# One K panel instead of two in combined form in the up projection of a streaming encoder layer

## Chip, cores and metric

The kernel runs on one core of a Trainium2 chip. The metric is the device time of one execution in microseconds (us). Engines are named as in the profile: PE is TensorE (matmuls; PEld its weight loads), DVE is VectorE, ACT is ScalarE, POOL is GpSimd, SP is SyncE, which here only issues loads.

## What is computed

One layer of a hybrid encoder for 256 prompt frames of one stream and 16 frames each of 8 sample streams (384 rows in all, three tiles of 128): projections, a convolution branch and an attention branch, their gated sum through `w_out`, and then the part in which the change lies, a feed-forward block with a gated causal convolution:

```
h2 = rmsnorm(x, norm_ffn_g)
up = h2 @ w_up                      # 384 x 2048 times 2048 x 11264
g_half = up[..., :D_FF]             # D_FF = 5632
u_half = up[..., D_FF:]
ext_f = concatenate([ffn_buf, g_half], axis=1)
gc = causal_dwconv(ext_f, ffn_dw_w, ffn_dw_b)      # 3 taps
x = x + (silu(gc) * u_half) @ w_down
```

The last gate rows of each stream are outputs too (`prompt_ffn`, `sample_ffn`).

## The kernel before

**Precision and units.** A product of two float32 matrices is made of three matmuls: both operands are split into a high part and the rest (`hi`, `lo`), and hi·hi, hi·lo and lo·hi are added up in PSUM (L1154 to L1156, and L301 to L303 in `gemm`). A weight block of 256 rows by 512 columns (512 KB) is loaded by SP into a raw buffer (`fetch`, L127), and `split` (L146) makes its halves: `hi` on ACT (L155), then `lo` on DVE (L156), which frees the raw buffer. There are five raw buffers in the feed-forward block (three named `raw`, and S0 and S1 of an older pool) and three pairs of `hi` and `lo` (two and `third`). `ahead` (L255) keeps up to `depth` splits issued ahead of their matmuls. Every engine works through its own queue in order; a scheduler sets the order within a queue by priorities at build time.

**The up projection** runs in 11 column groups (`up_group`, L1165). Group g makes 512 gate columns and 512 up columns of all 384 rows. K = 2048 is cut into four panels q of 512, each of two halves of 256. The groups alternate with the down projection: up 0, 1, 2, down, up 3, 4, down, and so on, so that the profile has five up stages (of 3, 2, 2, 2 and 2 groups).

**Plain panels** take their four weight blocks as they are: `pu0`, `pu1` (up columns, K halves 0 and 1) and `pg0`, `pg1` (gate columns), each for three row tiles and two K tiles of 128. One such item is 18 matmuls, a panel 72.

**Panels in combined form** (`MIXED = (0, 1)`) use a scheme of Strassen's kind for the 256 prompt rows. With the four blocks B11, B21 (gate columns, K halves 0 and 1) and B12, B22 (up columns), seven products take the place of eight. The items, in the code's names:

| item | what is split | loads | products | matmuls |
|---|---|---|---|---|
| b22 | B22 | B22 | q3, sample up | 12 |
| t3 | sums = B22 + B12 (L197) | B12 | p7, sample up | 12 |
| t1 | B11 + B12, in place (L202) | B11 | p5 | 6 |
| b11 | B11 | B11, a second time | p1, sample gate | 12 |
| t2 | sums = sums + B11 (L206) | | q6 | 6 |
| b21 | B21 | B21 | sample gate, p2 | 12 |
| t4 | sums = sums + B21 (L206) | | q4 | 6 |

The 128 sample rows have four plain products in these items. A panel is 66 matmuls, five loads and seven splits. The activations' combinations (`xm`) are made once, after `w_out`. q3, p2 and q4, and the up rows' second accumulator q2, go on to collect the plain panels; p5, p7, p1 and q6 are combined with them when they leave PSUM, on ACT and DVE (L1190 to L1225). There are five PSUM banks for these (`acc`) and three more (`misc`).

**After a group,** the up rows and the gate rows are turned to columns (DVE transposes L315, POOL's DMAs L320 and L325 through DRAM), the gate rows get their taps (L1124, L1126), and `product` (L1132 to L1136) makes the halves for the down projection. These follow in `tick`s, one for every nine matmuls.

`steps` (L172) sets the order of a group's items. In groups 1 to 10 the items of the panels 0 and 1 are spread among the eight plain ones; group 0 takes the six up items of both panels first.

Of the kernel before, what the change touches and what calls it, by code (L numbers as in the profile page):

```python
# [33 lines left out]
SPLIT_AHEAD, EVAC_AHEAD, FFN_AHEAD = 150, 60, 250  # L34
MIXED = (0, 1)

# [5 lines left out]
def hybrid_step(  # L42
# [23 lines left out]
    gp, close_gp = pool("acts")  # L66
    acc, close_acc = pool("acc", bufs=5, space=PSUM)
# [56 lines left out]

    fetched, wide = [], [False]
# [18 lines left out]
    third = []  # L144

    def split(raw, o, by_row=False):  # L146
        if third and len(third) % 3 == 0:
            hi, lo = third[0]
# [3 lines left out]
        if third:  # L152
            third.append(0)
        for k in (slice(0, 1), slice(1, 2)) if by_row else (slice(0, 2),):
            nc.scalar.copy(hi[:, k, :o], raw[:, k, :o])  # L155
            tt(lo[:, k, :o], raw[:, k, :o], f(hi[:, k, :o]), op=ALU.subtract)  # L156
        return hi, lo
# [14 lines left out]
    def steps(first):  # L172
        def spread(heavy, plain):
            n, m = len(heavy), len(plain)
            return [x for i in range(n) for x in [heavy[i]] + plain[i * m // n:(i + 1) * m // n]]

        up = [(what, q) for q in MIXED for what in ("b22", "t3", "t1")]
        top = [(what, q) for q in MIXED for what in ("b11", "t2")]
        low = [(what, q) for q in MIXED for what in ("b21", "t4")]
        pu, pg = ([(f"p{side}{h}", q) for q in PLAIN for h in range(2)] for side in "ug")  # L180
        if first:
            return up + pu[:-2] + top[:-2] + pu[-2:] + top[-2:] + spread(low, pg)
        return spread(up, pu) + spread(top + low, pg)

    def planned_mixed(w, c1, c2, first):
        held = {}

        def add(fn):
            plan.append(lambda: split(fn(), 512))

        def single(name, k, c):
            held[name] = fetch([rows_of(w, k, c, 512)])[0]
            return held[name]

        def both(q):
            sums[q] = new_sum[0](q)
            tt(sums[q], held["b22"][:], single("b12", 4 * q, c2)[:], op=ALU.add)  # L197
            return sums[q]

        def top(q):  # L200
            b = single("b11", 4 * q, c1)
            tt(b[:], b[:], held["b12"][:], op=ALU.add)  # L202
            return b

        def grown(q, name):
            tt(sums[q], sums[q], held[name][:], op=ALU.add)  # L206
            return sums[q]

        make = {"b22": lambda q: single("b22", 4 * q + 2, c2), "t3": both, "t1": top,
                "b11": lambda q: single("b11", 4 * q, c1), "t2": lambda q: grown(q, "b11"),  # L210
                "b21": lambda q: single("b21", 4 * q + 2, c1), "t4": lambda q: grown(q, "b21")}
        for what, q in steps(first):
            if what[0] == "p":
                planned(w, 4 * q + 2 * int(what[2]), [({"u": c2, "g": c1}[what[1]], 512)], 2)
            else:
                add(lambda what=what, q=q: make[what](q))
# [61 lines left out]
    def gemm(jobs, sides=()):  # L278
        for js in jobs:
# [4 lines left out]
            for j, k in [(j, k + i) for k in range(0, js[0]["nk"], 2) for j in js for i in range(2)]:  # L284
# [19 lines left out]
                if sp:  # L304
                    with tc.high_priority(offset=FFN_AHEAD if wide[0] else EVAC_AHEAD):
                        for m in range(nb):
                            j["evac"](m, ps[m])
                    if "done" in j:
                        j["done"]()
# [661 lines left out]
    p_x2, close_x2 = pool("x2")  # L971
    third_parts = [p_x2.tile([P, 2, 512], F32R, name=n)[:] for n in ("hi3", "lo3")]
    xg = {q: p_x2.tile([P, 2, 4, NT], F32R, name=f"xg{q}") for q in range(4) if q not in MIXED}
# [15 lines left out]

    def block():  # L990
        return p_w.tile([P, NTT * 512], F32, tag="block", bufs=4, name="block")

# [89 lines left out]
    plain_sums = gp.tile([P, 3, 2, 512], F32, tag="G0", name="sums")  # L1082
    third.append(third_parts)
# [6 lines left out]
    def up_g_done(g, box):  # L1090
        def done():
            cs = slice(512 * g, 512 * (g + 1))
            rows = box[0].rows
# [3 lines left out]
            gd = box[0].moved().rearrange("p i t q c -> p (i t) q c")  # L1097

# [44 lines left out]

    def run(seq, forms, finish):
        last = {b: (i, n) for i, prods in enumerate(seq) for n, (b, _, _) in enumerate(prods)}
        for i, prods in enumerate(seq):
            ahead(depth[0])
            hi, lo = ready.pop(0)
            for n, (b, (ah, al), kk) in enumerate(prods):
# [6 lines left out]
                mm(o, al, hi[:, kk, :], start=False, stop=last[b] == (i, n))  # L1156
            for b in last:
                if last[b][0] == i:
                    finish[b](forms[b][:])
            spent[0] += len(prods)  # L1160
# [4 lines left out]
    def up_group(g):  # L1165
# [12 lines left out]
        def rows(name):  # L1178
            if name not in box:
                for n in ("u", "g"):  # L1180
                    box[n] = block()[:].rearrange("p (t n) -> p t n", t=NTT)
            return box[name]

        def out(fn):
# [4 lines left out]

        def p5(ps):  # L1190
            nc.scalar.activation(e0, ps, AF.Identity, scale=scale[0])
            nc.scalar.activation(e1, ps, AF.Identity, scale=scale[1])

        def p7(ps):
            nc.scalar.activation(rows("g")[:, 1], ps, AF.Identity, scale=scale[1])  # L1195

        def q3(ps):
            stt(rows("u")[:, 0], ps, scale[0], e0, op0=ALU.mult, op1=ALU.subtract)

        def q2(ps):  # L1200
            u = rows("u")[:, 1]
            with tc.high_priority(offset=FFN_AHEAD):
                stt(u, ps, scale[1], e1, op0=ALU.mult, op1=ALU.subtract)
            tt(u, u, rows("g")[:, 1], op=ALU.subtract)
# [4 lines left out]
        def p1(ps):  # L1209
            nc.scalar.copy(e1, ps)  # L1210
            nc.scalar.activation(rows("g")[:, 0], ps, AF.Identity, scale=scale[0])

        def q6(ps):
            with tc.high_priority(offset=FFN_AHEAD):
                tt(e0, ps, e1, op=ALU.subtract)
            for r, sc in ((rows("u")[:, 0], scale[0]), (rows("u")[:, 1], scale[1]),
                          (rows("g")[:, 1], nr2[:, 1:2])):
                stt(r, e0, sc, r, op0=ALU.mult, op1=ALU.add)
            ups[g] = Turned(block, rows("u")).moved().rearrange("p i t q c -> p (i t) q c")

# [3 lines left out]
        def q4(ps):  # L1224
            stt(rows("g")[:, 1], ps, scale[1], rows("g")[:, 1], op0=ALU.mult, op1=ALU.add)  # L1225

# [4 lines left out]
               if what[0] == "p" else pairs(q, *made[what]) for what, q in steps(g == 0)]  # L1231
        run(seq, forms, dict(p5=out(p5), p7=out(p7), q3=out(q3), q2=q2, tu=sample("u"),
                             p1=out(p1), q6=q6, p2=out(p2), q4=out(q4), tg=sample("g")))
        up_g_done(g, [Turned(block, rows("g"))])()

# [81 lines left out]
```

## Time and profile before

| what | us |
|---|---|
| median of 3 runs | 2016.13 (2009.7 to 2018.01) |
| the profiled execution | 2013.98 |
| its span, first to last instruction | 2012.3 |
| five up stages begin at | 912.4, 1185.5, 1384.3, 1581.0, 1778.8 |
| five down stages begin at | 1120.2, 1319.0, 1515.8, 1713.5, 1909.7 |

The mean clock granted to TensorE is 0.997 of full speed. In the profile, a group of instructions has its line, engine and operation, output and inputs by the program's names, count, busy time and mean, then the idle time of its engine just before, and what ended it. A row of the timeline has start, length, engine, line, and in brackets the wait ahead of it. A row of waits has the waiter, what it waited for, total, count, longest. A row of windows has the stretch, its length, and each engine's busy time with its count of instructions.

### The profile page before, as it was taken

Reading aid. Unit: us, or ns where it says so; the run is one execution under the profiler, and the core shown is the slowest. Engines: PE = TensorE matmul, PEld = TensorE weight load, DVE = VectorE, ACT = ScalarE, POOL = GpSimd, SP = SyncE. Lnnn points to the kernel's source line nnn. Section 1 sums busy time; section 2 is a strip of 40 time slices with the busy share of each in tenths; the row PEclk is TensorE's granted clock in tenths of the full one; section 3 lists DMA queues with packets and bytes.
Section 4 is the critical chain, followed back from the end, with each engine's and each line's share of the span. In section 5 each row is a group of like instructions: output and inputs, shape, how many; then the busy total and the mean of one; then the engine's idle time right before and its main releaser. Section 6 shows DMA issues by size and latency. Waiting matters only on the chain.

```text
span 2012.3 us, 24838 instructions
## 1 busy us (share of the span) xinstructions
PE 1972.1 (98%) x9254; PEld 1649.8 (82%) x9254; DVE 1267.4 (63%) x1692; ACT 893.4 (44%) x1308; POOL 261.0 (13%) x527
## 2 busy tenths in 40 slices
PE   9999999999999999999899999999999999999999
PEld 9999888888888888887777887788778877887787
DVE  4478889646556356557588647754775467556853
ACT  5433354554426223455355534543454445443541
POOL 1001121100000002101121200230112012201210
PEclk9999999999999999999999999999999999999999
DMA  6555776664444458667655775576557655776563
GB/s 182 159 170 158 234 226 216 203 178 133 129 126 126 128 179 269 207 215 217 202 154 184 209 201 158 167 218 198 164 175 221 188 182 163 219 209 192 171 204 115
DMA packets 200884, 369.74 MB, mean 184 GB/s; under 512 B 16738, under 2 KB 66909, under 8 KB 200755
## 3 DMA queue, kind: packets, MB, share of 16 engines
q1 hardware_dynamic: 178763, 284.32, 45.2%
q0 software_dynamic: 21680, 83.70, 14.8%
q8 instruction: 72, 1.18, 0.2%
q14 instruction: 49, 0.40, 0.1%
q10 hardware_dynamic: 320, 0.14, 0.0%
HBM read 313.32 MB, written 55.24 MB: 183 GB/s over the span
## 4 chain that ended last, share of the span: by engine, by line
PE 76%; DVE 10%; DMA 9%; issue 3%; ACT 1%; POOL 1%; DVEq 0%; SPq 0%; POOLq 0%
PE acc L301 17%; PE acc L302 17%; PE acc L303 17%; DMA raw<-in_w_up_dram 7%; DVE lo L156 5%; PE acc L1155 4%; PE acc L1156 4%; PE acc L1154 4%; PE misc L1156 2%; PE misc L1155 2%; PE misc L1154 2%; PE acc L298 2%; PE acc L296 1%; PE acc L297 1%; DVE ut L566 1%
## 5 line engine op out<-in xcount | busy, mean ns | idle before, releaser
L155 ACT CAST hi<-raw 128x1024 fp32r<-128x1024 f32 (+2 forms) x481 | 498.0, 1037 | 879.7 <-PE acc L303 470.3
L156 DVE TENSOR_TENSOR lo<-raw,hi 128x1024 fp32r<-128x1024 f32 (+2 forms) x481 | 576.2, 1202 | 470.5 <-ACT hi L155 469.7
L301 PE MATMUL acc<-hi,hT 128*128 128x512 f32 (+1 forms) x704 | 270.4, 384 | 0.1
L302 PE MATMUL acc<-lo,hT 128*128 128x512 f32 (+1 forms) x704 | 265.6, 377 | 0.5 <-DVE lo L156 0.5
L303 PE MATMUL acc<-hi,hT 128*128 128x512 f32 (+1 forms) x704 | 265.6, 377 | 0.0
L1155 PE MATMUL acc<-lo,xg 128*128 128x512 f32 x440 | 174.4, 396 | 20.8 <-DVE lo L156 20.7
L301 PE MATMUL acc<-hi,act 128*128 128x512 f32 x484 | 188.3, 389 | 0.0
L302 PE MATMUL acc<-lo,act 128*128 128x512 f32 x484 | 188.3, 389 | 0.0
L303 PE MATMUL acc<-hi,act 128*128 128x512 f32 x484 | 188.3, 389 | 0.0
L1154 PE MATMUL acc<-hi,xg 128*128 128x512 f32 x440 | 171.8, 390 | 1.2 <-ACT block L1195 1.0
L1156 PE MATMUL acc<-hi,xg 128*128 128x512 f32 x440 | 171.6, 390 | 0.6 <-DVE xg L1047 0.6
L566 DVE SCALAR_TENSOR_TENSOR ut<-ext,cw,ut 128x384 f32<-128x384 f32 x240 | 149.4, 623 | 5.5
L301 PEld LDWEIGHTS acc<-hi,hT 128*128 128x128 f32 x704 | 132.2, 188 | 24.1 <-issue 1.8
L302 PEld LDWEIGHTS acc<-lo,hT 128*128 128x128 f32 x704 | 132.3, 188 | 23.4 <-DVE lo L156 2.2
L303 PEld LDWEIGHTS acc<-hi,hT 128*128 128x128 f32 x704 | 132.1, 188 | 22.8
L320 POOL DMA_DIRECT2D turn<-block x124 | 69.1, 564 | 589.0 <-DVE block L315 586.2
L1155 PE MATMUL acc<-lo,xm 128*128 128x512 f32 x308 | 121.7, 395 | 3.3 <-DVE lo L156 3.3
L1155 PEld LDWEIGHTS acc<-lo,xg 128*128 128x128 f32 x440 | 82.7, 188 | 48.5 <-DVE lo L156 32.0
L1154 PE MATMUL acc<-hi,xm 128*128 128x512 f32 x308 | 121.1, 393 | 0.0
L1156 PE MATMUL acc<-hi,xm 128*128 128x512 f32 x308 | 120.9, 393 | 0.0
L303 PEld LDWEIGHTS acc<-hi,act 128*128 128x128 f32 x484 | 90.8, 188 | 18.9
L301 PEld LDWEIGHTS acc<-hi,act 128*128 128x128 f32 x484 | 90.8, 188 | 18.9
(350 smaller groups left out, 3436.1 us busy)
## 6 DMA issues: line engine op xcount, KB each, us to landing
raw<-in_w_up_dram SPq DMA_DIRECT2D x198, 512.0 KB
raw<-in_w_in_dram SPq DMA_DIRECT2D x96, 512.0 KB
raw<-in_w_down_dram SPq DMA_DIRECT2D x88, 512.0 KB
turn<-block POOLq DMA_DIRECT2D x120, 192.0 KB, 5.0
block<-turn POOLq DMA_DIRECT2D x30, 768.0 KB, 6.0
raw<-in_w_in_dram SPq DMA_DIRECT2D x64, 256.0 KB
raw<-in_w_out_dram SPq DMA_DIRECT2D x32, 512.0 KB
y_rows<-part POOLq DMA_DIRECT2D x16, 768.0 KB, 6.8
```

What stands on the lines that cost most here:

```text
L155: nc.scalar.copy(hi[:, k, :o], raw[:, k, :o])
L156: tt(lo[:, k, :o], raw[:, k, :o], f(hi[:, k, :o]), op=ALU.subtract)
L296: mm(o, hi[:, kk, s], ah, start=st, stop=False)
L298: mm(o, lo[:, kk, s], ah, start=False, stop=sp)
L301: mm(o, ah[:, s], hi[:, kk, :n], start=st, stop=False)
L302: mm(o, ah[:, s], lo[:, kk, :n], start=False, stop=False)
L303: mm(o, al[:, s], hi[:, kk, :n], start=False, stop=sp)
L320: nc.gpsimd.dma_start(d[:, :, i, :].rearrange("j r n -> r j n"), src[32 * i:32 * i + 32, :].rearrange("r (j n) -> r j n", j=4))
L566: stt(o, v, wc, o, op0=ALU.mult, op1=ALU.add)
L1154: mm(o, ah, hi[:, kk, :], start=st, stop=False)
L1155: mm(o, ah, lo[:, kk, :], start=False, stop=False)
L1156: mm(o, al, hi[:, kk, :], start=False, stop=last[b] == (i, n))
```

## The change

`MIXED` is `(0,)`: panel 0 stays in combined form, panel 1 is plain, with its own `xg1`. Along with it:

- B11 is loaded once. `across` adds it into B12's buffer (t1), the item b11 splits it, and t2's sum reads it; before it was loaded again for b11.
- Seven raw buffers: S2 and S3 as well, from a group's ninth load on in group 0 and odd groups, throughout in even ones. The down stages write through S2 and S3 and keep five. Buffers are taken in turn from a list.
- Four pairs of halves, `depth` 4.
- The order of a group is b22, t3, t1, (pu0), b11, t2, the other up items, pg0, b21, t4, pg1 and the other gate items. In group 0 no plain item stands among the first five.
- The products are combined when q6 is there: `q6` forms both up rows' start and e1 (for the gate rows); `q3` and `q2` finish the up rows at the end of the up items, which are then turned at once, ahead of the gate items. p5's PSUM bank is held until then, p1's until `out_p1`. The banks are handed out by a list in the order in which they come free.
- Up and gate rows share one row buffer (block 2) and one work buffer (block 3).

```diff
-MIXED = (0, 1)
+MIXED = (0,)
+ROOM, SPARE = 8, 2
...
+    banks, bank_of = list(range(5)), {}
     def acc_tile():
-        return acc.tile([P, 512], F32, tag="acc", name="acc")
+        n = banks.pop(0)
+        t = acc.tile([P, 512], F32, tag=f"acc{n}", name="acc")
+        bank_of[id(t)] = (n, t)
+        return t
+    def freed(*tiles):
+        banks.extend(bank_of.pop(id(t))[0] for t in tiles if id(t) in bank_of)
...
-    def fetch(srcs, by_row=False):
-        n = len(fetched)
-        fetched.append(0)
-        if wide[0] and n % 5 > 2:
-            raw = p_sg.tile([P, 2, 512], F32, tag=f"S{n % 5 - 3}", name="raw")
+    def fetch(srcs, by_row=False, more=0):
+        ok = ["raw"] + (["S0", "S1", "S2", "S3"][:2 + more] if wide[0] else [])
+        slot = next(s for s in slots if s in ok)
+        slots.remove(slot)
+        slots.append(slot)
+        if slot != "raw":
+            raw = p_sg.tile([P, 2, 512], F32, tag=slot, name="raw")
...
+        n = splits[0] % depth[0] - 2
+        splits[0] += 1
+        if n >= 0:
+            hi, lo = pairs_more[n]
...
-    depth[0] = 3
+    depth[0] = 2 + SPARE
...
+        top, low = [], pg[:1]
+        for q in MIXED:
+            top += [(what, q) for what in ("b22", "t3", "t1")] + ([] if first else [pu.pop(0)])
+            top += [(what, q) for what in ("b11", "t2")]
+            low += [("b21", q), ("t4", q)] + pg[len(low) // 3 + 1:len(low) // 3 + 2]
+        return top + pu + low + pg[len(MIXED) + 1:]
...
+        def load(rows):
+            count[0] += 1
+            return fetch([rows], more=2 if count[0] > room else 0)[0]
...
-        def top(q):
-            b = single("b11", 4 * q, c1)
-            tt(b[:], b[:], held["b12"][:], op=ALU.add)
+        def across(q):
+            b = held["b12"][:]
+            tt(b, b, single("b11", 4 * q, c1)[:], op=ALU.add)
             return b
...
-                "b11": lambda q: single("b11", 4 * q, c1), "t2": lambda q: grown(q, "b11"),
+                "b11": lambda q: held["b11"], "t2": lambda q: grown(q, "b11"),
...
-            planned_mixed(w_up, 512 * g, DFF + 512 * g, g == 0)
+            planned_mixed(w_up, 512 * g, DFF + 512 * g, g == 0, ROOM if g % 2 or g == 0 else 0)
...
-        def p5(ps):
-            nc.scalar.activation(e0, ps, AF.Identity, scale=scale[0])
-            nc.scalar.activation(e1, ps, AF.Identity, scale=scale[1])
...
+        def q6(ps):
+            tt(e0, ps, e0, op=ALU.subtract)
+            stt(e1, e0, neg[1], e1, op0=ALU.mult, op1=ALU.add)
+            u = rows("u")
+            nc.scalar.activation(u[:, 0], e0, AF.Identity, scale=scale[0])
+            stt(u[:, 1], forms["p5"][:], neg[1], e1, op0=ALU.mult, op1=ALU.subtract)
+            stt(u[:, 0], forms["p5"][:], neg[0], u[:, 0], op0=ALU.mult, op1=ALU.add)
+            freed(forms["p5"])
...
+        def up_done():
+            ups[g] = turned_rows("u", 0)
+            after(4, out_p1)
```

Two places show what the build makes of it. The first is DVE's queue at the join of groups 1 and 2, before: group 1's last sums and halves, the evacuation of its gate rows (L1222, L1225), and group 2's first items. Here `raw_8646` and `raw_8658` are B22 and B12 of panel 0, `raw_8723` is its B11, `raw_8766` and `raw_8779` are B22 and B12 of panel 1, the other `raw` tiles plain blocks.

```order
L202 TENSOR_TENSOR raw_8723<-raw_8723,raw_8658 128x1024
L156 TENSOR_TENSOR lo_8631<-raw_8628,hi_8630 128x1024
L156 TENSOR_TENSOR lo_8649<-raw_8646,hi_8648 128x1024
L156 TENSOR_TENSOR lo3_6749<-sums_7732,hi3_6748 128x1024
L1222 SCALAR_TENSOR_TENSOR block_8340<-acc_8483,r2_6760,block_8340 128x512
L1225 SCALAR_TENSOR_TENSOR block_8340<-acc_8487,r2_6760,block_8340 128x512
L197 TENSOR_TENSOR sums_7732<-raw_8766,raw_8779 128x1024
L156 TENSOR_TENSOR lo_8706<-raw_8703,hi_8705 128x1024
```

After the change, the same join. `raw_8567` and `raw_8589` are now B22 and B12, `raw_8612` is B11, and `raw_8509`, `raw_8519` and `raw_8543` are the last gate items of group 1.

```order
L213 TENSOR_TENSOR raw_8589<-raw_8589,raw_8612 128x1024
L167 TENSOR_TENSOR lo4_6751<-raw_8509,hi4_6750 128x1024
L167 TENSOR_TENSOR lo_8522<-raw_8519,hi_8521 128x1024
L167 TENSOR_TENSOR lo_8546<-raw_8543,hi_8545 128x1024
L167 TENSOR_TENSOR lo3_6749<-raw_8567,hi3_6748 128x1024
L167 TENSOR_TENSOR lo4_6751<-sums_7723,hi4_6750 128x1024
L217 TENSOR_TENSOR sums_7723<-sums_7723,raw_8612 128x1024
L167 TENSOR_TENSOR lo_8616<-raw_8589,hi_8615 128x1024
L1244 SCALAR_TENSOR_TENSOR block_8507<-acc_8465,r2_6761,block_8507 128x512
L1247 SCALAR_TENSOR_TENSOR block_8507<-acc_8469,r2_6761,sums_7723 128x512
```

Group 2's sums for t3, t1 and t2 now all stand ahead of the evacuation that ends group 1, with three plain halves between them; the first sum of a second panel is gone.

The second place is DVE's queue right behind that, in the changed kernel: pu0 of group 2 (`raw_8659`), b11, t2, the sum for t4 with B21 (`raw_8869`), and pu1 (`raw_8705`), pu0 of panel 2 (`raw_8730`).

```order
L328 STREAM_TRANSPOSE block_8640<-block_8507 128x4x4x32 x3
L167 TENSOR_TENSOR lo_8662<-raw_8659,hi_8661 128x1024
L167 TENSOR_TENSOR lo3_6749<-raw_8612,hi3_6748 128x1024
L167 TENSOR_TENSOR lo4_6751<-sums_7723,hi4_6750 128x1024
L217 TENSOR_TENSOR sums_7723<-sums_7723,raw_8869 128x1024
L167 TENSOR_TENSOR lo_8708<-raw_8705,hi_8707 128x1024
L167 TENSOR_TENSOR lo_8733<-raw_8730,hi_8732 128x1024
```

The sum that reads B21 has moved ahead of the halves of pu1, although its item, t4, comes seven items later than pu1.

More of the change, by code (lines that the diff above doesn't have):

```diff
@@ L66, in hybrid_step @@
     gp, close_gp = pool("acts")
-    acc, close_acc = pool("acc", bufs=5, space=PSUM)
+    acc, close_acc = pool("acc", space=PSUM)
     misc, close_misc = pool("misc", bufs=3, space=PSUM)
+    banks, bank_of = list(range(5)), {}
     def acc_tile():
-        return acc.tile([P, 512], F32, tag="acc", name="acc")
+        n = banks.pop(0)
[4 more added lines that the diff above has]
+        banks.extend(bank_of.pop(id(t))[0] for t in tiles if id(t) in bank_of)
     def misc_tile():
@@ L172, in steps, with planned_mixed @@
     def steps(first):
[L173 to L179, printed above, removed]
-        pu, pg = ([(f"p{side}{h}", q) for q in PLAIN for h in range(2)] for side in "ug")
[L181 to L186, printed above, removed]
+        pu, pg = ([(f"p{side}{h}", q) for q in PLAIN for h in range(2)] for side in "ug")
+        top, low = [], pg[:1]
[4 more added lines that the diff above has]
+        return top + pu + low + pg[len(MIXED) + 1:]
+    def planned_mixed(w, c1, c2, first, room):
+        held, count = {}, [0]
+        def load(rows):
+            count[0] += 1
+            return fetch([rows], more=2 if count[0] > room else 0)[0]
         def add(fn):
@@ L191, in single @@
         def single(name, k, c):
-            held[name] = fetch([rows_of(w, k, c, 512)])[0]
+            held[name] = load(rows_of(w, k, c, 512))
             return held[name]
@@ L213, in planned_mixed @@
             if what[0] == "p":
-                planned(w, 4 * q + 2 * int(what[2]), [({"u": c2, "g": c1}[what[1]], 512)], 2)
+                k, c = 4 * q + 2 * int(what[2]), {"u": c2, "g": c1}[what[1]]
+                add(lambda k=k, c=c: load(rows_of(w, k, c, 512)))
             else:
@@ L307, in gemm @@
                             j["evac"](m, ps[m])
+                    freed(*ps)
                     if "done" in j:
@@ L971, in hybrid_step @@
     p_x2, close_x2 = pool("x2")
-    third_parts = [p_x2.tile([P, 2, 512], F32R, name=n)[:] for n in ("hi3", "lo3")]
+    spare = [[p_x2.tile([P, 2, 512], F32R, name=f"{n}{i}")[:] for n in ("hi", "lo")] for i in range(3, 3 + SPARE)]
     xg = {q: p_x2.tile([P, 2, 4, NT], F32R, name=f"xg{q}") for q in range(4) if q not in MIXED}
@@ L988, in load_y, with block @@
             nc.gpsimd.dma_start(y[n][:, 2, :], xin[2][:, cs])
-    def block():
-        return p_w.tile([P, NTT * 512], F32, tag="block", bufs=4, name="block")
+    blocks_used = [0]
+    def block(n=None):
+        blocks_used[0] += n is None
+        return p_w.tile([P, NTT * 512], F32, tag=f"block{blocks_used[0] % 4 if n is None else n}", name="block")
     def combined(n, d):
@@ L1082, in hybrid_step @@
     plain_sums = gp.tile([P, 3, 2, 512], F32, tag="G0", name="sums")
-    third.append(third_parts)
+    pairs_more.extend(spare)
     wide[0] = True
-    depth[0] = 3
+    depth[0] = 2 + SPARE
     e0, e1 = plain_sums[:, 2, 0], plain_sums[:, 2, 1]
@@ L1088, in hybrid_step, with up_g_done @@
     scale = [r2[:, t:t + 1] for t in range(NTT)]
-    def up_g_done(g, box):
+    neg = [nr2[:, t:t + 1] for t in range(NTT)]
+    def up_g_done(g, rows, gd):
         def done():
             cs = slice(512 * g, 512 * (g + 1))
-            rows = box[0].rows
             nc.gpsimd.dma_start(prompt_ffn[0, 0, :, cs], rows[126:128, 1, :])
@@ L1142, in hybrid_step, with run @@
     spent = [0]
-    def run(seq, forms, finish):
+    def run(seq, forms, finish, then):
         last = {b: (i, n) for i, prods in enumerate(seq) for n, (b, _, _) in enumerate(prods)}
@@ L1156, in run @@
                 mm(o, al, hi[:, kk, :], start=False, stop=last[b] == (i, n))
-            for b in last:
-                if last[b][0] == i:
-                    finish[b](forms[b][:])
+            done = [b for b in finish if last[b][0] == i and finish[b]]
+            for b in done:
+                finish[b](forms[b][:])
+                freed(forms[b])
+            for b in done:
+                if b in then:
+                    then[b]()
             spent[0] += len(prods)
@@ L1179, in rows, with turned_rows @@
             if name not in box:
-                for n in ("u", "g"):
-                    box[n] = block()[:].rearrange("p (t n) -> p t n", t=NTT)
+                box[name] = block(2)[:].rearrange("p (t n) -> p t n", t=NTT)
             return box[name]
+        def turned_rows(name, n):
+            return turned(rows(name), block(3)[:], block(n)[:]).rearrange("p i t q c -> p (i t) q c")
         def out(fn):
@@ L1224, in q4 @@
         def q4(ps):
-            stt(rows("g")[:, 1], ps, scale[1], rows("g")[:, 1], op0=ALU.mult, op1=ALU.add)
+            stt(rows("g")[:, 1], ps, scale[1], e1, op0=ALU.mult, op1=ALU.add)
         made = {"b22": (("q3", 2), ("tu", 4)), "t3": (("p7", 3), ("tu", 8)), "t1": (("p5", 0),),
@@ L1231, in up_group @@
                if what[0] == "p" else pairs(q, *made[what]) for what, q in steps(g == 0)]
-        run(seq, forms, dict(p5=out(p5), p7=out(p7), q3=out(q3), q2=q2, tu=sample("u"),
-                             p1=out(p1), q6=q6, p2=out(p2), q4=out(q4), tg=sample("g")))
-        up_g_done(g, [Turned(block, rows("g"))])()
+        run(seq, forms, dict(p5=None, p7=out(p7), q3=out(q3), tu=sample("u"), q2=out(q2), p1=out(p1), q6=out(q6),
+                             p2=out(p2), tg=sample("g"), q4=out(q4)), {"q2": up_done})
+        up_g_done(g, rows("g"), turned_rows("g", 1))()
     def down_jobs(gs, last):
```

34 lines of the change are left out of this document (10 added, 24 removed).

## The prediction

> **What bounds the kernel now.** I read the page first, then the busy time of each engine stage by stage.
>
> ```profile
> span 2012.3 us, 24838 instructions
> PE 1972.1 (98%) x9254; PEld 1649.8 (82%) x9254; DVE 1267.4 (63%) x1692; ACT 893.4 (44%) x1308; POOL 261.0 (13%) x527
> ```
>
> TensorE (PE) looks full, but its busy time hides waits, because one matmul's record (0.39 us) is longer than the distance to the next. The windows view is cut here at the five up stages and one down stage; the weight loads (PEld) count the matmuls.
>
> ```profile
> core 0: us, PE busy (x) PEld busy (x) DVE busy (x) ACT busy (x) POOL busy (x), PEclk, DMA share, GB/s
> 912.40:1120.20 207.80, 194.72 (x829) 155.93 (x828) 152.21 (x180) 105.38 (x136) 35.36 (x78) 0.98 0.61 191
> 1120.20:1185.50 65.30, 65.30 (x289) 54.05 (x288) 32.14 (x38) 30.43 (x44) 12.59 (x28) 1.00 0.74 211
> 1185.50:1319.00 133.50, 127.14 (x553) 103.06 (x552) 92.69 (x101) 62.22 (x75) 19.95 (x35) 1.00 0.57 172
> 1384.30:1515.80 131.50, 127.34 (x554) 103.09 (x553) 92.91 (x101) 61.67 (x75) 16.77 (x35) 1.00 0.57 175
> 1581.00:1713.50 132.50, 128.43 (x553) 104.20 (x552) 92.73 (x101) 62.12 (x75) 18.79 (x35) 0.99 0.56 174
> 1778.80:1909.70 130.90, 126.92 (x553) 103.06 (x552) 92.86 (x101) 61.70 (x75) 17.53 (x37) 1.00 0.58 182
> ```
>
> The down stage runs 288 matmuls in 65.30 us: 0.2267 us from start to start, with nothing lost. The five up stages hold 828 + 4 x 552 = 3036 matmuls (the x553 is one at the edge), worth 3036 x 0.2267 = 688.4 us. They take 207.8 + 133.5 + 131.5 + 132.5 + 130.9 = 736.2 us. So **47.8 us are lost in the up stages**: 20.1 in the first, 5.8 to 8.4 in each other. That is all that this change can win back. The waits say on whom:
>
> ```profile
> DVE raw L202 <- DMA raw<-in_w_up_dram: 69.8, 21, 6.1
> DVE sums L206 <- DMA raw<-in_w_up_dram: 62.6, 28, 4.9
> PEld acc L1155 <- DVE lo L156: 37.8, 34, 3.1
> DVE sums L197 <- DMA raw<-in_w_up_dram: 30.7, 15, 4.3
> PE acc L1155 <- DVE lo L156: 24.1, 28, 2.7
> ```
>
> TensorE waits for a low half (L156) from VectorE (DVE). VectorE waits in turn, at the sums, for weights still on their way. At the join of two groups its queue reads, in order of time:
>
> ```profile
> 1441.45 1.22 DVE L202 TENSOR_TENSOR raw<-raw 128x1024 f32<-128x1024 f32 x1 [3.92 <-DMA raw<-in_w_up_dram]
> 1442.60 2.35 DVE L156 TENSOR_TENSOR lo<-raw,hi 128x1024 fp32r<-128x1024 f32 x2
> 1444.87 1.22 DVE L156 TENSOR_TENSOR lo<-sums,hi 128x1024 fp32r<-128x1024 f32 x1
> 1452.40 1.23 DVE L197 TENSOR_TENSOR sums<-raw 128x1024 f32<-128x1024 f32 x1 [3.65 <-DMA raw<-in_w_up_dram]
> 1453.55 1.22 DVE L156 TENSOR_TENSOR lo<-raw,hi 128x1024 fp32r<-128x1024 f32 x1
> ```
>
> And the chain of work that ended last, at this place and at an earlier one:
>
> ```profile
> 1007.67 3.67 DMA raw<-in_w_up_dram
> 1444.98 7.33 DMA raw<-in_w_up_dram
> ```
>
> This is a loop. A low half ends at 1444.9 and frees a raw buffer; the load into it lands 7.33 us later; the sum that needs it stands at the head of VectorE's queue for 3.65 us; the low half behind it (1453.55) is the one TensorE lacks:
>
> ```profile
> 1453.30 0.39 PE L1154 MATMUL acc<-hi,xg 128*128 128x512 f32 x1
> 1454.82 0.50 PE L1155 MATMUL acc<-lo,xg 128*128 128x512 f32 x1 [1.13 <-DVE lo L156]
> ```
>
> So the up stages are bound by the way from a freed buffer through load and split, not by the rate of transfers: the DMA share is 0.57 there and 0.74 in the down stage that loses nothing.
>
> **What the change adds.** Panel 1 becomes plain: 72 matmuls for 66 in each of 11 groups, 66 more (8,921 rows on TensorE for 8,855). Priced by spacing: 66 x 0.2267 = **+15.0 us**, all of it on the path. [...]
>
> **What it removes.** Per group, by these rows:
>
> ```profile
> L156 DVE TENSOR_TENSOR lo<-raw,hi 128x1024 fp32r<-128x1024 f32 x456 | 555.2, 1222 | 448.8 <-ACT hi L155 448.1
> L155 ACT CAST hi<-raw 128x1024 fp32r<-128x1024 f32 x456 | 479.6, 1053 | 851.8 <-PE acc L303 448.0 <-PE acc L1156 182.9 <-PE misc L1156 81.7
> L206 DVE TENSOR_TENSOR sums<-sums,raw 128x1024 f32<-128x1024 f32 x44 | 53.9, 1225 | 62.8 <-DMA raw<-in_w_up_dram 62.6
> L1218 DVE SCALAR_TENSOR_TENSOR block<-sums,r,block 128x512 f32<-128x512 f32 x22 | 15.6, 749 | 0.0
> L1191 ACT ACTIVATE sums<-acc,r 128x512 f32<-128x512 f32 x11 | 7.5, 686 | 2.1 <-PE acc L1156 2.1
> L315 DVE STREAM_TRANSPOSE block<-block 128x512 f32<-128x512 f32 x66 | 43.5, 692 | 0.0
> raw<-in_w_up_dram SPq DMA_DIRECT2D x198, 512.0 KB
> ...
> y_rows<-y POOLq DMA_DIRECT2D x4, 768.0 KB, 3.9
> ```
>
> Splits go from 22 to 19, each 1.05 us of ScalarE (ACT) and 1.22 of VectorE. Sums go from 8 to 4, each 1.225. VectorE thus has 3 x 1.22 + 4 x 1.225 = 8.6 us less of 62.6, and one evacuation less (0.75); ScalarE has 3.2 us less and one evacuation less (0.69). Loads go from 18 to 16 (198 to 176 in all): one in 4.0 us instead of 3.5. None of this is on TensorE's path by itself; it is worth what it takes off the 47.8 us.
>
> **What it moves.** In the times below, an item's TensorE time is its matmuls by 0.2267: 4.08 us plain, 2.72 (b22, t3, b11, b21) or 1.36 (t1, t2, t4).
> - *Split pairs, three to four.* A split can begin when the item that last used its pair is done. Before, two items lie between that and the need, at least 4.08 us (b11 and t2). After, it is three, at least 6.80 (b22, t3, t1 ahead of pu0). A split is 1.05 + 1.22 = 2.3 us, so 1.8 us were left for anything ahead in VectorE's queue; now 4.5.
> - *Raw buffers, five to seven, and where they are held.* In the plain stretches the release of a buffer is now 5 to 7 items of 4.08 us ahead of its next need, 20 us and more against a landing of 3.67 to 7.33 us. Next to the combined items it is less. The tightest is B21, which takes pu0's buffer. Taking a group's start as zero: pu0's low half stands behind two evacuations (0.75) and three transposes (0.69) and takes 1.22 itself: 4.8, say 5.0 us with the signals, and its buffer is free. The sum for t4, which reads B21, stands ahead of pu1's low half, which TensorE needs at 14.96. Take off 1.14 for that sum and 1.14 for the low half (their distance in the rows above), and B21 must land by 12.7: 7.7 us after its issue, against the longest 7.33. No wait by these rows, with 0.4 us to spare at worst and 4 at best.
> - *Taps and products* stay where they were in ticks; the eight scaled adds and eight products of a group fall into the plain stretch, where a split has 10 us and more. I cost them at nothing; if the cover went, each would delay a split by about 0.6 us.
> - *PSUM.* The five banks go round in the order of release. p5's bank is held until q6 is there; t1 of the next group takes p2's bank 5.4 us after p2 ends, against one scaled add of 0.75. Nothing, or 0.5 us a group at most.
> - *The gate rows and the earlier turn of the up rows* add no transfer; the turn comes at the end of the up items, some 28 us ahead of the next group. Nothing; at worst it meets loads, which is in the range.
> - *At the start,* loads for pu5 and pg0 go into buffers 2 and 3 of the old y panels and stand on SP's queue ahead of the last w_out loads. They wait for a y panel's write (3.9 us to landing), while the w_out loads behind them run an item of 4.08 us and more ahead of their need: nothing, up to 3.9 us.
>
> **What stays lost.** In the first group, t3's split comes behind the last panel's squares on ScalarE (about 1.1 us), and panel 3's halves come no earlier than now:
>
> ```profile
> 936.52 0.62 ACT L1043 ACTIVATE block<-block,col 128x384 f32<-128x384 f32 x1
> 940.52 0.55 DVE L1047 TENSOR_TENSOR xg<-block,xg 128x384 fp32r<-128x384 f32 x1
> ```
>
> They are ready at 941.1. The new order wants them after 120 matmuls, 27.2 us, at 912.4 + 1.1 + 27.2 = 940.7: about 1 us with the next piece. That makes 2.5 for this group. For the ten others I take 0.5 each, between nothing (the slacks above) and the 2.7 to 4.2 that they lose now (5.8 to 8.4 per pair), near the lower end because each slack above is positive. With 0.5 for joins: 2.5 + 5.0 + 0.5 = **8 us**.
>
> Part of the present loss follows from the long waits:
>
> ```profile
> 966.67 0.39 PE L1154 MATMUL misc<-hi,xm 128*128 128x512 f32 x1
> 971.28 0.80 PE L1155 MATMUL misc<-lo,xm 128*128 128x512 f32 x1 [4.22 <-DVE lo L156]
> 971.87 0.63 PE L1156 MATMUL misc<-hi,xm 128*128 128x512 f32 x1
> 972.30 0.63 PE L1154 MATMUL misc<-hi,xm 128*128 128x512 f32 x1
> 1661.26 0.50 PE L1155 MATMUL acc<-lo,xm 128*128 128x512 f32 x1 [2.09 <-DVE lo L156]
> 1662.53 0.63 PE L1154 MATMUL acc<-hi,xm 128*128 128x512 f32 x1
> 1662.95 0.63 PE L1155 MATMUL acc<-lo,xm 128*128 128x512 f32 x1
> ```
>
> After a wait of 4.22 us the matmuls stand 0.43 us apart, half speed, and again from 1662.53 after one of 2.09. [...]
>
> **Sum,** against the profiled execution (2013.98 us, span 2012.3): 2013.98 + 15.0 - (47.8 - 8.0) = 2013.98 - 24.8 = 1989.2. The median of the runs shown, 2016.13, lies 2.2 above that execution; I forecast 1990, 1.3% below the median. A measurement tells about 0.5% (10 us) of this kernel from no change.
>
> **Rivals.**
> 1. *The sums still wait for loads at the joins,* because the turned blocks share the transfers (the sums are still ahead of low halves on VectorE, as the rows show). Then half of the loss stays, 24 us: 2013.98 + 15.0 - 23.8 = 2005. For it: 0.57 of the DMA engines are busy on average. Against: fewer loads, and each asked for earlier.
> 2. *Slower: B21's wait takes the place of the old one.* The t4 sum at the head of VectorE's queue holds pu1's low half in every group. It costs what the landing takes beyond 7.7 us. The gain is gone at (47.8 - 15.0 - 8.0) / 11 = 2.3 us a group, a landing of 10.0 us (10 us more to be told from no change: 10.9); at 11.5 us it is 3.8 x 11 = 41.8, so 1989.2 + 41.8 = 2031. For it: the sum stands there in every group, with the turn of the last group's gate rows in flight. Against: 7.33 us is the longest such piece in the chain.
> 3. *The pairs and buffers don't matter and the loss stays as it is:* 2013.98 + 15.0 = 2029. It would need another cause than the loop above; no row shows one.
>
> **How the numbers follow.** Forecast, 3 to 16 us lost (1984 to 1997): 0.76. Rival 1 (1997 to 2013): 0.15, of which two thirds below 2006. Rivals 2 and 3: 0.06. Better than 1984: 0.03. The range 1983 to 2004 leaves out the upper half of rival 1 and the slower cases. Faster: 0.76 + 0.03 + 0.10 = 0.89; same 0.06; slower 0.05.
>
> **What would show it.** The up stages would have 846 and 564 matmuls, 191.8 and 127.9 us by spacing, and last some 195 and 129. The waits of VectorE's sums for loads (163 us now) may remain in part; those of the second matmul of each three (L1155 now) for low halves, 37.8 and 24.1 us now, should fall below 12 together. No stretch of half speed should be left in the first stage. It would be wrong if the 564 matmuls took 131 us or more, with low halves behind a waiting sum.

## The result and the profile after

| | before | after |
|---|---|---|
| median, us | 2014.43 (4 runs, 2009.7 to 2018.01) | 1981.24 (4 runs, 1980.63 to 1982.25) |
| profiled execution, us | 2013.98 | 1980.66 |
| span, us | 2012.3 | 1979.0 |
| lost in the five up stages, us | 47.8 | 0.0 |

The ratio is 0.9837, interval 0.9815 to 0.986: 1.6% faster, 33 us. Three executions in the experiments below (2807.69 us of run 7, 2506.37 of run 11 and 2195.89 of run 13) had a mean granted clock of 0.65, 0.73 and 0.85, all others 0.99 or more, and nothing below uses them.

From the page of the changed kernel, the span, the busy times and the chain that ended last, by engine:

```profile
span 1979.0 us, 24788 instructions
PE 1970.4 (100%) x9320; PEld 1663.5 (84%) x9320; DVE 1176.5 (59%) x1597; ACT 854.4 (43%) x1262; POOL 260.6 (13%) x527
PE 98%; DVE 1%; DMA 0%; issue 0%; POOL 0%; ACT 0%; SPq 0%; POOLq 0%; DVEq 0%
```

The chain of before had 19% on VectorE and loads:

```profile
PE 76%; DVE 10%; DMA 9%; issue 3%; ACT 1%; POOL 1%; DVEq 0%; SPq 0%; POOLq 0%
```

It is now TensorE almost from end to end. The windows of the changed kernel, cut at the five up stages (the second row is a down stage), with the columns of the view of before:

```profile
912.35:1104.11 191.76, 191.76 (x847) 158.84 (x846) 128.07 (x156) 94.02 (x124) 39.06 (x78) 1.00 0.61 195
1104.11:1169.39 65.28, 65.28 (x289) 54.07 (x288) 33.24 (x39) 30.71 (x44) 12.06 (x27) 1.00 0.68 190
1169.39:1297.23 127.84, 127.84 (x565) 105.89 (x564) 75.95 (x84) 54.95 (x67) 18.45 (x35) 1.00 0.57 176
1362.51:1490.35 127.84, 127.84 (x565) 105.89 (x564) 75.94 (x84) 54.96 (x67) 18.46 (x35) 1.00 0.57 175
1555.63:1683.47 127.84, 127.84 (x565) 105.89 (x564) 75.97 (x84) 54.96 (x67) 18.43 (x35) 1.00 0.58 175
1748.75:1876.59 127.84, 127.84 (x565) 105.89 (x564) 75.94 (x84) 54.94 (x67) 20.59 (x39) 1.00 0.61 192
```

846 + 4 x 564 = 3102 matmuls by 0.2267 are 703.2 us, and the stages last 191.76 + 4 x 127.84 = 703.1. PE is busy for the whole of each, at full clock. VectorE's waits for loads of the up projection, from the view of waits, are 26.3 us (163.1 before; the two longest rows follow, the third is 0.7), and the matmul that lacked low halves waits for nothing (last number, view by lines):

```profile
DVE sums L208 <- DMA raw<-in_w_up_dram: 13.1, 6, 2.9
DVE sums L217 <- DMA raw<-in_w_up_dram: 12.5, 9, 2.9
```

```profile
L1170 PE MATMUL acc<-lo,xg 128*128 128x512 f32 x660 | 256.7, 389 | 0.0
```

### The profile page after: what moved, and what is told of

The parts are those of the page before. It is cut to its first block, busy times and chain, and to the rows that moved or that the text cites. A ratio compares the mean times of both kernels' runs of the same rounds, so it can differ in the third digit from the quotient of the medians.

```text
span 1979.0 us, 24788 instructions
## 1 busy us (share of the span) xinstructions
PE 1970.4 (100%) x9320; PEld 1663.5 (84%) x9320; DVE 1176.5 (59%) x1597; ACT 854.4 (43%) x1262; POOL 260.6 (13%) x527
## 3 DMA queue, kind: packets, MB, share of 16 engines
q0 software_dynamic: 21680, 83.70, 15.3%
## 4 chain that ended last, share of the span: by engine, by line
PE 98%; DVE 1%; DMA 0%; issue 0%; POOL 0%; ACT 0%; SPq 0%; POOLq 0%; DVEq 0%
PE acc L313 17%; PE acc L314 17%; PE acc L315 17%; PE acc L1169 9%; PE acc L1170 9%; PE acc L1171 9%; PE misc L1169 3%; PE misc L1170 3%; PE misc L1171 3%; PE acc L310 2%; PE acc L308 2%; PE acc L309 2%; PE misc L313 1%; PE misc L314 1%; PE misc L315 1%; DVE ut L579 1%
## 5 line engine op out<-in xcount | busy, mean ns | idle before, releaser
L1169 PE MATMUL acc<-hi,xg 128*128 128x512 f32 x660 | 256.7, 389 | 0.0
L1170 PE MATMUL acc<-lo,xg 128*128 128x512 f32 x660 | 256.7, 389 | 0.0
L1171 PE MATMUL acc<-hi,xg 128*128 128x512 f32 x660 | 256.7, 389 | 0.0
L1169 PEld LDWEIGHTS acc<-hi,xg 128*128 128x128 f32 x660 | 123.9, 188 | 25.7
L1171 PEld LDWEIGHTS acc<-hi,xg 128*128 128x128 f32 x660 | 123.9, 188 | 25.7
L1170 PEld LDWEIGHTS acc<-lo,xg 128*128 128x128 f32 x660 | 123.9, 188 | 25.6
L315 PEld LDWEIGHTS acc<-hi,act 128*128 128x128 f32 x484 | 90.9, 188 | 18.9
L314 PEld LDWEIGHTS acc<-lo,act 128*128 128x128 f32 x484 | 90.9, 188 | 18.8
```

What stands on the lines that cost most here:

```text
L314: mm(o, ah[:, s], lo[:, kk, :n], start=False, stop=False)
L315: mm(o, al[:, s], hi[:, kk, :n], start=False, stop=sp)
L1169: mm(o, ah, hi[:, kk, :], start=st, stop=False)
L1170: mm(o, ah, lo[:, kk, :], start=False, stop=False)
```

## The experiments

**How they are compared.** By the span of the profiled execution, unless a median is given, and by the loss in the up stages: their lengths, less 0.2267 us for each matmul (3036 with two combined panels, 703.2 us' worth with one). A span is that of one execution. Runs 2, 3 and 4 were timed once; the four timings of run 1 spread over 5.1 us, the two of run 14 over 7.0, and in both the profiled one is the lowest. So among the kernels with two panels a difference of under some 5 us between two rows is not shown. The last two columns come from the timelines of VectorE and ScalarE between 905 us and the end of the last up stage: how long the sums waited for a load, and in how much of that time a low half behind the sum in the queue already had its high half (the n-th cast on ScalarE belongs to the n-th low half on VectorE). Run 9 has no sums. Runs 4, 10, 11 and 13 stand in the text alone.

| run | panels | order | raw buffers, B11 loads | sums | span | lost | sums wait | ready low half behind |
|---|---|---|---|---|---|---|---|---|
| before | 2 | old | 5, two | whole | 2012.3 | 47.8 | 163.2 | 69.9 |
| 8 | 2 | old | 7, two | whole | 1997.3 | 31.3 | 111.9 | 47.1 |
| 7 | 2 | new | 5, two | whole | 1979.9 | 15.8 | 67.9 | 29.0 |
| 5 | 2 | new | 5, one | whole | 1974.7 | 11.1 | 68.8 | 26.9 |
| 6 | 2 | new | 7, two | whole | 1973.5 | 9.1 | 46.5 | 15.6 |
| 1 | 2 | new | 7, one | whole | 1970.0 | 6.2 | 44.9 | 15.0 |
| 2 | 1 | old | 5, two | whole | 1980.2 | 1.3 | 31.9 | 3.3 |
| 3 | 1 | new | 5, one | whole | 1979.0 | 0.2 | 46.7 | 16.3 |
| after | 1 | new | 7, one | whole | 1979.0 | 0.0 | 26.3 | 12.5 |
| 14 | 2 | old | 5, two | whole, in place | 1978.7 | 14.7 | 74.4 | 18.9 |
| 15 | 2 | old | 5, two | half, in place | 1969.8 | 4.5 | 85.9 | 21.8 |
| 12 | 2 | old | 5, two | one column | 1965.1 | 1.5 | 76.4 | 9.7 |
| 9 | 2 | old | 5, two | none | 1965.0 | 1.3 | - | - |

"New order" stands for all of the change but the panel, the buffers, the pairs and the load: the order of items, the sum for t1 made on B12, banks and evacuation. The last column does not rank the runs: run 3 holds ready low halves for 16.3 us and loses 0.2, run 14 for 18.9 and loses 14.7. The column does not tell whether TensorE needed the low half before the wait was over, nor what else stood between them.

**Runs 1 and 2: the panel, or all the rest.** Run 1 is the changed kernel with both panels combined (three pairs). Run 2 is the kernel before with one.

```diff
-MIXED = (0,)
-ROOM, SPARE = 8, 2
+MIXED = (0, 1)
+ROOM, SPARE = 8, 1
```

```diff
-MIXED = (0, 1)
+MIXED = (0,)
```

> The changed kernel with both panels 0 and 1 in combined form again (66 matmuls fewer: 3036 in the up stages, 688.4 us by spacing), with the new order, B11 loaded once, early combination, seven raw buffers, but three pairs of halves (a fourth does not fit beside two combined panels). Theory A (the loss of before came from the way of a freed buffer through load and split, so order and buffers cured it, whatever the number of panels): less than 12 us lost in the up stages, span 1979.0 - 15.0 + 0 to 12 = 1964 to 1976 us. Theory B (it came from the pace that two combined panels ask of loads and splits, 18 loads and 22 splits a group; the one panel cured it): 20 us and more stay lost, span 1984 us or more.

> The kernel before with one line changed: panel 1 plain, panel 0 combined. Old order, B11 loaded twice, five raw buffers, three pairs of halves. 3102 matmuls in the up stages, 703.4 us by spacing. Theory A: most of the loss stays, 20 us or more, so a span of 2000 us or more. Theory B: less than 8 us lost, span 1979 to 1987 us.

The first and second up stage of run 1, then of run 2, in the windows view:

```profile
912.00:1104.60 192.60, 189.30 (x830) 154.94 (x828) 151.08 (x177) 102.69 (x133) 36.49 (x78) 1.00 0.59 191
1169.88:1295.23 125.35, 125.35 (x553) 103.53 (x552) 91.46 (x98) 60.87 (x73) 16.72 (x35) 1.00 0.57 175
```

```profile
912.45:1105.59 193.14, 192.10 (x848) 158.70 (x846) 130.02 (x159) 94.06 (x127) 35.82 (x79) 1.00 0.63 199
1170.87:1298.71 127.84, 127.84 (x566) 105.86 (x565) 78.83 (x88) 54.94 (x69) 16.19 (x35) 1.00 0.59 184
```

The spacing gives 187.7 and 125.1 for two panels, 191.8 and 127.9 for one. Each half of the change is nearly enough alone: the panel takes the loss to 1.3 us, the rest takes it to 6.2. Together they paid twice, and the panel's 66 matmuls had to be paid for. Run 1 has a median of 1973.99 us (1971.73 to 1976.85, 4 runs), ratio 0.98 (0.9783 to 0.9818), below the changed kernel.

**Runs 3 and 4: buffers and pairs under one panel.** Run 3 is the changed kernel with five raw buffers and three pairs, run 4 with three pairs alone (`SPARE = 1`).

> The changed kernel with five raw buffers and three pairs of halves, as before; the new order, B11 loaded once and the one panel stay. Theory A: 10 us or more come back as loss (span 1989 or more). Theory B: under 4 us (span under 1983). Order and single load as the cure: here under 4 us, but 15 us or more in the old scheme with one panel.

> The changed kernel with three pairs of halves, seven raw buffers. Theory A, by the shortest stretch between two uses of a pair (two items of 4.08 us together, against 2.3 us for a split): 3 to 10 us lost, span 1982 to 1989. Theory B: under 2 us, span under 1981.

Spans 1979.0 and 1978.8, against 1979.0, with 0.2 and 0.8 us lost. With one panel and the new order, the two buffers and the fourth pair are worth nothing that shows.

**Runs 5 to 8: what of the rest counts, with two panels.** Run 5 closes the two buffers, run 6 loads B11 twice, run 7 does both. Run 8 gives the kernel before seven buffers, by the new `fetch`.

```diff
-"b11": lambda q: held["b11"],
+"b11": lambda q: single("b11", 4 * q, c1),
```

> Two combined panels, the new order, B11 loaded once, three pairs, but five raw buffers in place of seven. The run with two panels and seven buffers had a span of 1970.0 us, with some 6 us lost in the up stages (gaps there on TensorE beyond 0.2267 us a matmul); the kernel before loses 47.6 us. Theory 'buffers': the two more raw buffers gave most of the 41 us, so here over 20 us are lost, span 1985 to 2010. Theory 'single load': the load of B11 that is saved gave it, so five buffers suffice, span 1968 to 1976. Theory 'order': the order in which the sums and loads stand gave it, span 1968 to 1976 too; the last two are told apart by the next two runs.

> Two combined panels, the new order, seven raw buffers, three pairs, but B11 loaded twice, as before: 18 loads a group in place of 16. Theory 'single load': the loss comes back, over 20 us, span 1985 to 2010. Theories 'buffers' and 'order': at most 6 us more than the 1970.0 of the run with one load, span 1968 to 1978.

> Two combined panels, three pairs, five raw buffers and B11 loaded twice, as before; what is left of the change is the order of the items, the sum formed on B12 in place of B11, the output banks and the evacuation. Theory 'order': most of the gain stays, span 1968 to 1982. Theories 'buffers' and 'single load': the loss is back, span 1995 to 2015.

> The kernel before with seven raw buffers in place of five and nothing else: two combined panels, old order, B11 twice, three pairs, the same 9252 matmuls. Theory 'buffers', and the prediction's own (the way from a freed buffer through load and split): loads land earlier, most of the 47.6 us goes, span 1968 to 1990 against about 2012.5. Theories 'order' and 'single load': under 12 us go, span 2000 to 2013, and the sums on VectorE still wait for loads at the head of its queue.

The first two up stages of run 7, the new order alone, in the windows view:

```profile
912.09:1106.45 194.36, 189.79 (x829) 154.81 (x828) 150.81 (x177) 102.51 (x133) 35.33 (x78) 1.00 0.64 208
1171.73:1299.14 127.41, 126.36 (x553) 103.24 (x552) 90.95 (x98) 61.45 (x73) 16.16 (x35) 1.00 0.60 189
```

Runs 5, 6 and 7 fall into the bands of "order". The new order, with neither the buffers nor the single load, takes 32.0 of the 47.8; no run parts what this name stands for (the items, the sum on B12, banks and evacuation). From run 7 to run 1, the buffers and the load are worth 9.6 us together; alone, the buffers 6.7 (run 6) and the load 4.7 (run 5), each near the spread of the timings. In the old order the two buffers take 16.5: in the four later stages 27.8 became 11.5, the first still loses 19.8. So run 8 falls between its two bands; the order is the largest part, the buffers and the load come behind it, and none carries all. Run 8 also shows plainly how low halves are held. VectorE's queue, then ScalarE's, then TensorE's:

```profile
965.65 0.74 DVE L1210 SCALAR_TENSOR_TENSOR block<-acc,r,sums 128x512 f32<-128x512 f32 x1
970.57 1.23 DVE L208 TENSOR_TENSOR raw<-raw 128x1024 f32<-128x1024 f32 x1 [4.18 <-DMA raw<-in_w_up_dram]
...
974.90 1.89 DVE L322 STREAM_TRANSPOSE block<-block 128x512 f32<-128x512 f32 x3
976.71 2.32 DVE L158 TENSOR_TENSOR lo<-raw,hi 128x1024 fp32r<-128x1024 f32 x2
```

```profile
968.37 1.99 ACT L157 CAST hi<-raw 128x1024 fp32r<-128x1024 f32 x2
```

```profile
972.00 0.39 PE L1161 MATMUL misc<-hi,xm 128*128 128x512 f32 x1
977.95 0.80 PE L1162 MATMUL misc<-lo,xm 128*128 128x512 f32 x1 [5.56 <-DVE lo L158]
978.54 0.63 PE L1163 MATMUL misc<-hi,xm 128*128 128x512 f32 x1
978.97 0.63 PE L1161 MATMUL misc<-hi,xm 128*128 128x512 f32 x1
```

The two high halves are done at 970.4. Their low halves stand behind a sum that waited 4.18 us for its load, and behind the evacuations and transposes that queued up with it; they come at 976.7, and TensorE, at the matmul that reads the first of them, waits 5.56 us. Of the 6.3 us in which they were ready, the sum's wait makes 0.2 and its work 1.1; the other five go to what stands between the sum and them in the queue. In the kernel before, too, VectorE ran the eight rows of its queue at the join of groups 1 and 2 in the order of the queue, from 1047.18 to 1058.91 us.

**Runs 9, 12, 14, 15: the sums themselves.** All are the kernel before, with its order, buffers, loads and splits. Run 9 has no sums; in 12, 15 and 14 they are made in place, 1, 256 and 512 columns wide. None of the four computes the layer.

```diff
+        def touch(b, other):
+            tt(b[:, :, 0:1], b[:, :, 0:1], other[:, :, 0:1], op=ALU.add)
+            return b
...
         def both(q):
-            sums[q] = new_sum[0](q)
-            tt(sums[q], held["b22"][:], single("b12", 4 * q, c2)[:], op=ALU.add)
-            return sums[q]
+            return touch(single("b12", 4 * q, c2), held["b22"])
```

> The kernel before with the eight sums a group left out: T3 is split from B12 alone, T1 and T2 from B11, T4 from B21. Two panels, the old order, five raw buffers, three pairs, and the same 18 loads, 22 splits and 9252 matmuls; B12's buffer comes free some items earlier. Theory 'sums' (the prediction's chain: a sum at the head of VectorE's queue waits for its load and holds back the low half behind it): most of the loss goes, under 15 of 47.6 us are left in the up stages, span under 1982. Theory 'pace' (18 loads through five buffers and 22 splits through three pairs are too many for 62.6 us of matmuls, sums or no sums): over 30 us are left, span over 1995. In between, both count.

> The kernel before with each of the eight sums a group shrunk to one column of 512 and made in place: they read the same loads and hold the same buffers, but cost VectorE next to nothing (two panels, old order, five raw buffers, B11 twice, three pairs). Without the sums the loss went from 47.6 us to about 1. Theory 'waits and holds': a sum that waits at the head of the queue, or that keeps B12's buffer, makes the loss, whatever its length, so over 25 us are left, span over 1990. Theory 'work': the 1.22 us of each sum, 9.8 us a group, on VectorE make it, so under 12 us are left, span under 1977.

> As the run with sums of one column, with nothing changed but their width: all 512 columns, 1.22 us each, in place (T3 on B12's buffer, T2 and T4 on B11's and B21's, so the tile for the sums isn't used, and what T1 to T4 hold are not the sums of the computation). The narrow ones lost about 1 us. Theory 'work': the length of the sums makes the loss, which comes back: over 25 us, span over 1990. Theory 'sums tile': the chain through the separate tile of sums (T2's sum waits for T3's halves, T4's for T2's) or the program's other order made it, so under 10 us are lost, span under 1975.

> As the run before with 256 of 512 columns, some 0.65 us a sum (in place, not the sums of the computation). Theory 'work': between the two, 5 to 20 us lost, span 1969 to 1985; under 3 us if there is a threshold that the half width stays below. Theory 'sums tile': as the run before, within 3 us.

The sums of runs 12, 15 and 14 in the view by lines (count, busy time, ns of one, idle time ahead and what ended it):

```profile
L196 DVE TENSOR_TENSOR raw<-raw 128x2 f32<-128x2 f32 x88 | 14.1, 162 | 77.2 <-DMA raw<-in_w_up_dram 76.4
```

```profile
L196 DVE TENSOR_TENSOR raw<-raw 128x512 f32<-128x512 f32 x88 | 60.2, 689 | 86.6 <-DMA raw<-in_w_up_dram 85.9
```

```profile
L196 DVE TENSOR_TENSOR raw<-raw 128x1024 f32<-128x1024 f32 x88 | 107.0, 1221 | 74.9 <-DMA raw<-in_w_up_dram 74.4
```

The first two up stages of run 9, in the windows view:

```profile
911.87:1100.91 189.04, 188.00 (x830) 155.38 (x828) 129.83 (x158) 103.87 (x136) 38.39 (x79) 1.00 0.66 213
1166.19:1291.31 125.12, 125.12 (x554) 103.64 (x552) 78.04 (x87) 61.85 (x75) 17.19 (x35) 1.00 0.61 194
```

Run 9: two panels, 18 loads and 22 splits a group through five buffers and three pairs lose only 1.3 us once the sums are gone, so "pace" falls. The short sums wait 76.4 us for loads at the head of the queue and 1.5 us are lost: a wait there costs nothing by itself, so "waits and holds" falls. With 0.16, 0.69 and 1.22 us a sum the loss is 1.5, 4.5 and 14.7: the length counts, as "work" has it. Run 15's loss is just under its band of 5 to 20 us. But run 14 falls between its two bands: whole sums in place still lose 33 us less (26 by its other timing) than the kernel before, whose sums are as long and go to a tile of their own. In place, T2's and T4's sums write over what the low halves of B11 and B21 read, and so can't stand ahead of them; before, 67 of 88 sums had a low half behind them that was ready by the sum's end, in run 14 32. That this order makes the difference is argued from those counts; the queues differ in other places too, and no run changes it alone. Nor does the count rank the runs: run 15 has 31 and loses 4.5.

**Run 13: the sums on GpSimd,** in the kernel before.

```diff
-            tt(sums[q], held["b22"][:], single("b12", 4 * q, c2)[:], op=ALU.add)
+            nc.gpsimd.tensor_tensor(sums[q], held["b22"][:], single("b12", 4 * q, c2)[:], op=ALU.add)
```

> The kernel before with the eight sums a group made on GpSimd in place of VectorE, whole and from the same loads; nothing else is changed. Theory 'head of VectorE's queue': the sums' waits and work are off that queue, no low half stands behind a sum, so most of the loss goes, span 1965 to 1985. Theory 'holds': B12's and the first B11's buffers are held as long as before or longer, five buffers are too few, so over 30 us are left, span over 1995. If GpSimd takes over 4 us a sum, T1 and T2 come later by that and the run tells less.

The sums that grow, in the view by lines, and TensorE's wait in the view of waits:

```profile
L206 POOL TENSOR_TENSOR sums<-sums,raw 128x1024 f32<-128x1024 f32 x44 | 117.0, 2661 | 135.3 <-DMA raw<-in_w_up_dram 84.1 <-DVE lo L156 44.9 <-issue 6.2
```

```profile
PE misc L1154 <- ACT hi L155: 16.5, 6, 6.0
```

The span is 2033.7 and 70.8 us are lost: the band of "holds", not that of "head of VectorE's queue". A sum takes 2.66 us there and waits for low halves besides; TensorE now waits for high halves too. The sum itself is late here, so the run does not tell the queue from the buffers.

**Runs 10 and 11: the first group with two panels.** Run 1 with the two more buffers open in group 0 from the sixth load on, and from the fourth.

> Two combined panels with the rest of the change (three pairs), and in the first group the two more raw buffers are open from the sixth load on and not from the ninth. The run with two panels lost 5.0 us in the first stage and 1.2 us in the four others; some 3 us of the 5.0 stand at loads of the second panel (gaps at 926, 934.8 and 945 us). Theory 'buffers' for the first group: the sixth load is issued earlier, 1.5 to 3 us less than two panels with room 8, a median of 1970 to 1974. Rival: the two buffers are still held by what was in them before, or the order of the queue lets a later load wait, then no change, 1972 to 1977. Either way it is below the 1981.24 of the changed kernel, since 66 matmuls of 0.2267 us are saved and under 8 us are lost.

> As the run before, with the two more raw buffers open from the fourth load of the first group on. Theory 'buffers': all three waits of the first group's second panel shrink, a median of 1969 to 1973. Rival: these loads are now queued behind the last readers of the two buffers, and the first group's loads come later: 1974 to 1982.

Run 10: 1970.81 us (1970.44 to 1972.81, 5 runs), ratio 0.9773 (0.9748 to 0.9797). It is the fastest kernel here that computes the layer, 10.4 us below the changed one; its range overlaps that of run 1, so the earlier buffers themselves are not shown to help (3.1 us are lost in its first stage against 4.9 in run 1, but 2.8 against 1.3 in the others). Run 11 has a median of 1978.77 (3 runs): the rival was right, 12.1 us are lost in its first stage, 4.5 of them in one gap.

## Why the prediction came out as it did

The sum was right in all terms but one. **The term "what stays lost", 8 us, measured 0.0.** Without it the sum is 2013.98 + 15.0 - 47.8 = 1981.2, against 1980.66 in the profiled execution. The range was wrong for the same reason: its end at 1983 kept nearly 2 us of the loss, and "better than 1984" had 0.03.

- *The first group, 2.5 predicted, 0.0 measured.* The two pieces that the working names, 1.1 and about 1, make 2.1; it gives no source for the other 0.4. The split of t3 was put behind the last panel's squares on ScalarE, and panel 3's halves at 941.1. ScalarE and VectorE of the changed kernel:

```profile
911.92 0.60 ACT L1049 ACTIVATE acc<-y 128x512 f32<-128x512 f32 x1 [2.39 <-DVE y L1048]
912.61 1.05 ACT L166 CAST hi<-sums 128x1024 fp32r<-128x1024 f32 x1
913.56 0.59 ACT L1049 ACTIVATE acc<-y 128x512 f32<-128x512 f32 x1
```

```profile
913.70 1.23 DVE L167 TENSOR_TENSOR lo<-sums,hi 128x1024 fp32r<-128x1024 f32 x1
935.54 1.02 DVE L1063 TENSOR_TENSOR xg<-block,xg 128x384 fp32r<-128x384 f32 x2
937.90 1.02 DVE L1063 TENSOR_TENSOR xg<-block,xg 128x384 fp32r<-128x384 f32 x2
```

  The split went between the squares, not behind them, and its low half ended at 914.9, as b22's 2.72 us of matmuls ended (912.35 + 2.72 = 915.1). The panel's halves were done at 938.9, 2.2 us earlier than taken over from before, and ahead of 940.7.
- *The ten other groups, 0.5 each predicted, 0.0 measured.* The working had found each slack positive, and charged half a microsecond all the same. The slacks held, and nothing was lost. B21, the tightest, in group 2 (which starts at 1233.3):

```profile
1242.24 1.23 DVE L217 TENSOR_TENSOR sums<-sums,raw 128x1024 f32<-128x1024 f32 x1 [0.93 <-DMA raw<-in_w_up_dram]
1243.38 1.22 DVE L167 TENSOR_TENSOR lo<-raw,hi 128x1024 fp32r<-128x1024 f32 x1
```

  Its sum did wait at the head of the queue, until 8.9 us after the start; 12.7 was the bound, so 3.8 us are left, near the better of the two ends (0.4 and 4). So rival 2's sum stands where it said, and costs nothing.
- *Joins, 0.5:* nothing. Of rival 1's waits of sums for loads 26.3 us remain, and cost nothing.
- *66 matmuls, +15.0:* right. Run 9's span less its loss is 1963.7, the changed kernel's 1979.0: 15.3.
- *The loop and the low half behind a waiting sum:* the held low half is shown at one place by the rows of run 8, and that there is next to no loss without the sums by run 9. How the 47.8 us divide between the sums' waits, their work and their place in the queue is not shown. What was too narrow is the share that it gave to the parts. "The way from a freed buffer through load and split" needs the sum in it: loads and splits at the old pace lose 1.3 us without sums. And the panel was booked as a price, with its fewer sums and loads only as help to pairs and buffers, while it cures the loss alone (run 2) and leaves those nothing to do (runs 3 and 4). Rival 3 was right that they don't matter here, and wrong that the loss then stays.
- *What would show it:* the stages lasted 191.8 and 127.8 (some 195 and 129 predicted), the waits for low halves fell to nothing (below 12), and no half speed is left (granted clock 1.00 in each up stage).

Why one panel is enough in the old order is open: it halves the sums, spreads them and takes loads away, and no run parts these.

## What to carry to other kernels

When two cures come in one change, try each alone: here one cost 15 us of matmuls, and the other gave most of the gain without it. In these runs a sum that waited for its load at the head of VectorE's queue did no harm (76.4 us of such waits in run 12 go with 1.5 us lost) unless something that was ready and needed stood behind it; look for that pair in two timelines, not for the wait alone. And where a working finds the slack positive, put nothing lost into the range as a full case.

## What the runs showed of the hardware

Whether TensorE ran at half speed after a wait did not follow from the length of that wait. In the kernel before it did after a wait of 2.09 us (the prediction shows the rows at 1661.26), and in the same run it did not after 2.69:

```profile
1271.67 0.39 PE L1154 MATMUL acc<-hi,xg 128*128 128x512 f32 x1
1274.75 0.50 PE L1155 MATMUL acc<-lo,xg 128*128 128x512 f32 x1 [2.69 <-DVE lo L156]
1275.08 0.39 PE L1156 MATMUL acc<-hi,xg 128*128 128x512 f32 x1
1275.32 0.40 PE L1154 MATMUL acc<-hi,xg 128*128 128x512 f32 x1
```

The granted clock of that run is 0.50 from 969.60 us, within the wait of 4.22 us, to 976.42, and from 1662.50, 1.2 us after the end of the wait of 2.09, to 1665.91; between 7.04 and 2010.66 us it is otherwise 1.00. For the waits of 2.09 and 2.69 us, the stretch in which each ends and one behind it, with PE's busy time, the granted clock, and the DMA columns:

```profile
1659.09:1662.50 3.41, 1.32 (x6) 1.00 0.34 93
1662.50:1665.91 3.41, 3.41 (x9) 0.50 1.03 411
1273.38:1276.79 3.41, 2.04 (x9) 1.00 0.25 44
1276.79:1280.20 3.41, 3.41 (x17) 1.00 0.76 262
```

What tells the two waits apart is not shown. At the clock of 0.50 the matmuls start 0.43 us apart (from 971.87 to 976.14 and from 1662.53 to 1665.51), against 0.2267 in the down stage at 1.00. Behind the wait of 5.56 us in run 8 they start 0.43 us apart as well (978.54 and 978.97).
